# Layer 2's cross-attention output taken by token tile, with the next units' splits traced behind the norms

## The chip, the cores and the metric

The kernel runs on one core of one Trainium2 chip. The metric is the time of one execution on the device in microseconds (us); smaller is better. The core's engines work side by side, each through its own list of instructions in order: PE (the matrix engine, with its weight loads shown as PEld), DVE (vector), ACT (scalar and activation functions), POOL, and SP, whose queue issues the transfers from memory.

## The reference, cut to what matters

The program is an encoder of two layers over 256 tokens of width 1024, in float32. Each layer has a mixer, a cross-attention to a memory of 256 tokens and a feed-forward part (FFN), and each of the three ends in a residual with a layer norm:

```
for l in range(2):
    h = hybrid_mixer(x, ...)
    x = layer_norm(alpha * x + h, ln_g[l, 0], ln_b[l, 0])
    h = memory_cross_attention(x, mem, ...)        # softmax(q k^T) v, 4 heads, then o @ xa_o
    x = layer_norm(alpha * x + h, ln_g[l, 1], ln_b[l, 1])
    u, gt = split(x @ ffn_w_in)                    # 2 x 2816 columns
    h = (silu(dwconv(gt) + b) * u) @ ffn_w_out
    x = layer_norm(alpha * x + h, ln_g[l, 2], ln_b[l, 2])
```

What changes lies between `o @ xa_o` of the second layer and the first columns of its FFN.

## The kernel before, in words

**Tiles.** The 256 tokens are two tiles of 128 rows, `x[0]` and `x[1]` (tile 0 and tile 1 below; x_147 and x_148 in lists of instructions). A product against an activation needs it transposed, features on the partitions, so after each norm every 128x128 block of x is transposed by PE against an identity (`transp`, L455) into a PSUM bank `att` and copied out.

**Precision by splitting.** Each float32 operand is split in two: `hi` is the value rounded to the matrix engine's format (ACT's CAST, L276), `lo` is the rest (DVE's subtraction, L277). A product then takes three matmuls, hi·hi, hi·lo and lo·hi (`mm3`, L271 to L273).

**Units.** Weights come as units of 128x1024 (512 KB) in the fixed order in which the products use them. `prefetch` (called ahead of every step, up to `LOOK` = 7 units further than the step needs) issues a unit's transfer into one of 4 `raw` buffers from SP's queue and its split into one of 8 pairs of `hi` and `lo`. A raw buffer is free again when the unit's `lo` is done.

**Order.** A planner (`interleave`) merges generators of steps (the main line, norms, attention heads) by estimated costs, waits and free PSUM banks into one list, in which the code is traced. From the traced order a scheduler then builds each engine's list by its own estimates, so an engine's order differs locally from the traced one; SP's order is kept as traced. `add_manual_dep(..., NOSYNC)` only keeps two instructions of one engine in order.

**PSUM.** 3 banks `acc` and 5 banks `att`, each 128x512.

**The residual.** `tok_out` writes the output projection: first columns 0 to 511 of both tiles (two acc banks, units 0 to 3), then columns 512 to 1023 of tile 0 (an att bank, units 4 to 7), then the same columns of tile 1 in two pieces of 256. When a piece is complete, `ln_part` adds it to x (L391, on DVE) and takes its statistics (L396). `residual` starts the norm of tile 0 (`ln`) when `tail` = 4 steps are left, and that of tile 1 after the last. A norm is: BN_AGGR (L409), ACT's square root (L410), `sub` (L414, two pieces of 512 in tile 0, four of 256 in tile 1), a reciprocal (L426), `scale` (L419, same pieces), then the transposes (L455) and their splits into `hi` and `lo` (L276, L277).

**Behind it, in layer 2 only.** `keep_warm` (L1052) is a product of the identity with itself, 8 matmuls whose result nobody reads. `up_first` (units `fm`) computes the first 512 "up" columns of the FFN token by token, for tile 0 as soon as its transposes are there, then for tile 1. Then `ffn_in` takes the "gate" units `fg` 0 to 3 (columns 0 to 511, features on the partitions), each with 2 transposes of the finished up columns (L1080), and from column 512 on pairs of units `fu` and `fg`. Each unit's product is `proj_twin` (L299 to L303) into an acc bank, which `fold` empties (L307 on ACT, L308 on DVE). A gate unit then goes through a small convolution (L1090 on ACT, L1091, L1093 on DVE), silu (L1095, ACT) and the product with the up columns (L1096, DVE). The first silu of a layer is preceded by the load of silu's table into ACT.

## Time and profile before

| | |
|---|---|
| time, median of 3 runs | 1125.92 us (1124.89 to 1125.96) |
| the profiled execution | 1125.41 us; its span from first to last instruction is 1123.6 us |
| granted clock of the matrix engine, mean | 0.995 |
| busy share of the span | PE 98%, PEld 87%, DVE 74%, ACT 57%, POOL 1% |
| read from memory | 204.18 MB, 183 GB/s over the span |

Busy shares are of the whole span. A line such as L276 is a line of the kernel; helpers have one line for all their callers. In a timeline, a row gives the start in us from the span's start, the time until the last of the row's instructions ends, the engine, the line and operation, output and inputs by the program's names without numbers, how many, and in brackets how long the engine was idle before and what ended that. Matmuls overlap: one of 512 columns is listed with 0.39 us though the next starts 0.23 us later.

### The profile page before, as it was taken

To read this page: it belongs to the slowest core of one execution; us is meant where nothing else is said; L and a number is where in the kernel's file an instruction comes from. 1 tells how busy PE (TensorE), PEld (TensorE's weight loads), DVE (VectorE), ACT (ScalarE), POOL (GpSimd) and SP (SyncE) were. 2 spreads that over 40 slices of the span, in tenths; PEclk is the share of its full clock that TensorE was granted. 3 is DMA by queue.
4 is the path that set the end of the run, shared out by engine and by line. 5 is a ranking of instruction groups with operands and counts; after the bars stand their busy time and mean duration, and the time that the engine had idled before them with its cause. 6 is when DMAs were issued, how large, how long until landed. Compare 5 with 4: busy or idle time off the path is not lost.

```text
span 1123.6 us, 17442 instructions
## 1 busy us (share of the span) xinstructions
PE 1098.5 (98%) x6700; PEld 982.5 (87%) x6700; DVE 833.0 (74%) x1300; ACT 643.8 (57%) x1060; POOL 12.4 (1%) x18
## 2 busy tenths in 40 slices
PE   9999999999999999999999999999999978999997
PEld 8899998888998988888899999888889877888886
DVE  7888888567965898885487878865777576888744
ACT  5656667445554576665355667744536436666640
POOL 0000000000000000000000000000000000000001
PEclk9999999999999999999999999999999989999999
DMA  8884436657563575666747544656746344566651
GB/s 300 284 255 145 149 133 226 187 188 243 168 205 104 174 221 188 190 190 194 263 150 232 165 148 151 200 183 197 257 149 194 131 150 150 173 189 188 195 174 37
DMA packets 60466, 208.45 MB, mean 186 GB/s; under 512 B 7008, under 2 KB 8288, under 8 KB 60384
## 3 DMA queue, kind: packets, MB, share of 16 engines
q1 hardware_dynamic: 59952, 206.83, 57.2%
q8 instruction: 52, 0.85, 0.3%
q10 hardware_dynamic: 432, 0.52, 0.1%
q14 instruction: 30, 0.25, 0.1%
HBM read 204.18 MB, written 1.05 MB: 183 GB/s over the span
## 4 chain that ended last, share of the span: by engine, by line
PE 93%; DVE 3%; ACT 1%; DMA 1%; issue 1%; SPq 0%; DVEq 0%; ACTq 0%
PE acc L271 19%; PE acc L272 19%; PE acc L273 19%; PE acc L303 12%; PE acc L301 7%; PE att L272 4%; PE att L273 4%; PE att L271 4%; PE acc L299 2%; DVE lo L277 1%; DMA raw<-in_w_dram 1%; PE att L455 1%; PE att L666 1%; PE att L581 1%; PE att L580 1%
## 5 line engine op out<-in xcount | busy, mean ns | idle before, releaser
L277 DVE TENSOR_TENSOR lo<-raw,hi 128x1024 fp32r<-128x1024 f32 x355 | 432.3, 1223 | 187.0 <-ACT hi L276 181.9
L276 ACT CAST hi<-raw 128x1024 fp32r<-128x1024 f32 x355 | 371.4, 1051 | 224.0 <-PE acc L273 75.3
L272 PE MATMUL acc<-lo,big 128*128 128x512 f32 x584 | 229.5, 393 | 0.8 <-DVE lo L277 0.8
L271 PE MATMUL acc<-hi,big 128*128 128x512 f32 x584 | 229.4, 394 | 0.0
L273 PE MATMUL acc<-hi,big 128*128 128x512 f32 x584 | 226.7, 391 | 0.0
L271 PE MATMUL acc<-big,hi 128*128 128x256 f32 x704 | 200.2, 285 | 3.2 <-ACT big L335 2.4
L273 PE MATMUL acc<-big,lo 128*128 128x256 f32 x704 | 200.5, 285 | 0.6 <-DVE lo L277 0.6
L272 PE MATMUL acc<-big,hi 128*128 128x256 f32 x704 | 199.9, 284 | 0.2 <-DVE big L277 0.2
L303 PE MATMUL acc<-big,hi 128*128 128x512 f32 x588 | 149.2, 393 | 0.0
L271 PEld LDWEIGHTS acc<-big,hi 128*128 128x128 f32 x704 | 134.7, 192 | 4.4 <-ACT big L335 2.8
L273 PEld LDWEIGHTS acc<-big,lo 128*128 128x128 f32 x704 | 134.9, 192 | 1.2 <-DVE lo L277 1.0
L272 PEld LDWEIGHTS acc<-big,hi 128*128 128x128 f32 x704 | 134.9, 192 | 0.8 <-DVE big L277 0.4
L273 PEld LDWEIGHTS acc<-hi,big 128*128 128x128 f32 x584 | 110.0, 188 | 22.8
L272 PEld LDWEIGHTS acc<-lo,big 128*128 128x128 f32 x584 | 110.3, 189 | 21.0 <-DVE lo L277 1.1
L271 PEld LDWEIGHTS acc<-hi,big 128*128 128x128 f32 x584 | 110.1, 189 | 20.1 <-ACT t L823 0.2
L303 PEld LDWEIGHTS acc<-big,hi 128*128 128x128 f32 x588 | 105.1, 189 | 18.3
L301 PEld LDWEIGHTS acc<-big,lo 128*128 128x128 f32 x672 | 91.9, 190 | 6.7 <-ACT big L276 0.2
L301 PE MATMUL acc<-big,lo 128*128 128x256 f32 x672 | 94.1, 282 | 0.0
L272 PE MATMUL att<-lo,big 128*128 128x256 f32 (+1 forms) x228 | 72.6, 319 | 0.0
L271 PE MATMUL att<-hi,big 128*128 128x256 f32 (+1 forms) x228 | 72.4, 317 | 0.0
L273 PE MATMUL att<-hi,big 128*128 128x256 f32 (+1 forms) x228 | 72.3, 318 | 0.0
L307 ACT COPY t<-acc 128x256 f32<-128x256 f32 x84 | 31.2, 372 | 65.1 <-PE acc L303 65.1
(156 smaller groups left out, 1241.0 us busy)
## 6 DMA issues: line engine op xcount, KB each, us to landing
raw<-in_w_dram SPq DMA_DIRECT2D x355, 512.0 KB, 4.2
t<-in_bias_dram SPq DMA_DIRECT2D x16, 256.0 KB, 5.7
big<-in_ln_g_dram SPq DMA_DIRECT2D x6, 512.0 KB, 5.4
big<-in_ln_b_dram SPq DMA_DIRECT2D x6, 512.0 KB, 6.2
raw<-in_memT_dram SPq DMA_DIRECT2D x6, 512.0 KB, 4.6
big<-big SPq DMA_DIRECT2D x16, 128.0 KB, 2.3
x<-in_x_dram SPq DMA_DIRECT2D x4, 256.0 KB, 7.7
t<-in_memT_dram SPq DMA_DIRECT2D x3, 256.0 KB, 6.8
```

The costliest lines, as they stand in the source:

```text
L271: mm(o, lh, rh, start=first, stop=False)
L272: mm(o, lh, rl, start=False, stop=False)
L273: self.done = mm(o, ll, rh, start=False, stop=last)
L276: return (self.nc.scalar.copy(ah, src), self.nc.vector.tensor_tensor(out=al, in0=src, in1=rd(ah), op=ALU.subtract))
L277: self.nc.vector.tensor_tensor(out=al, in0=src, in1=rd(ah), op=ALU.subtract))
L299: mm(o, hi[:, 0], xa.both(0), start=True, stop=False)
L301: mm(o[:, S:], lo[:, k], xa.hi(k), start=False, stop=False)
L303: mm(o, hi[:, k], xa.both(k), start=False, stop=k == KT - 1)
L307: self.nc.scalar.copy(dst, o[:, S:])
L455: nc.tensor.transpose(pt[:, k], self.x[i][:, (n * h + k) * P:(n * h + k + 1) * P], self.ident)
L580: self.nc.tensor.matmul(o, q[m][:, h, t], k[m][:, h], start=True, stop=False)
L581: self.nc.tensor.matmul(o, q[m][:, h, t], k[2 + m][:, h], start=False, stop=True)
```

## The change

1. In layer 2, `tok_tiles` takes the place of `tok_out`: all 1024 columns of tile 0 first, then all of tile 1 (its last 512 columns again in two pieces of 256). `residual` gets tail = 12, so tile 0's norm is started when tile 0's eight steps are traced.
2. While that runs, `prefetch` is capped: the first cap (`until`) stands before unit fm 0, is moved to fg 0 at the start of tile 1's second half, and is lifted when `up_first` comes to tile 1 (`lift`). So the splits of fm 0 to 3, and of fg 0 on, are traced behind the norms' instructions. Tile 1's adds are kept behind the last scale of tile 0 on DVE (`behind`).
3. Silu's table: a silu of one column directly behind tile 1's square root, in both layers, in the norm ahead of the FFN.
4. `keep_warm` is gone.
5. In `ffn_in` the transposed up columns of fg 0 to 3 go into att banks instead of acc banks.

The diff, cut to its core:

```
+    def ln_part(self, i, c, acc=None, behind=False):
...
+            add = nc.vector.scalar_tensor_tensor(out=x[:, sl], in0=x[:, sl], scalar=ALPHA, in1=acc, ...)
+            if behind:
+                self.tc.add_manual_dep(add.ins, self.scaled, NOSYNC, reason="behind the first tile's norm")
+            self.urgent(add)
...
             self.urgent(nc.scalar.activation(rs, mv[:, 1:2], AF.Sqrt, bias=self.epsb, scale=1.0))
+            if i == 1 and nxt is not None and nxt[-1] == "2":
+                nc.scalar.activation(self.small(1), rs, AF.Silu)
...
-                    self.urgent(scale(h))
+                    self.scaled = self.urgent(scale(h)).ins.name
...
+    def until(self, unit):
+        self.cap = self.order.index(unit)
+
+    def lift(self, unit=None):
+        self.cap = len(self.order) if unit is None else self.order.index(unit)
+        self.prefetch(min(self.pos + self.LOOK, self.cap))
+
+    def tok_tiles(self, n, l, a):
...
+        for i in range(NT):
+            for h in range(2):
+                for c in ((0, 256), (256, 512)) if i == h == 1 else ((0, 512),):
+                    for q in range(4):
+                        def fn(*u, i=i, h=h, c=c, q=q):
...
+                            if i == h == q == 0:
+                                self.until(("fm", l, 0))
+                            if i == h == 1 and q == c[0] == 0:
+                                self.lift(("fg", l, 0))
+                            if q == 0:
+                                st["o"] = (self.acc() if h == 0 else self.att())[:, :c[1] - c[0]]
+                            part(q, i, h, c)
+                            if q == 3:
+                                self.ln_part(i, (512 * h + c[0], 512 * h + c[1]), st["o"], i == 1)
...
-            yield from self.residual(self.tok_out("xo", l, ("oT", l)), f"a{l}", xn)
             um = l == DEPTH - 1
             if um:
-                yield Step(self.keep_warm, acq=1, rel=1)
+                yield from self.residual(self.tok_tiles("xo", l, ("oT", l)), f"a{l}", xn, 12)
+            else:
+                yield from self.residual(self.tok_out("xo", l, ("oT", l)), f"a{l}", xn)
+            if um:
                 yield from self.up_first(l, xn, [f"a{l}0", f"a{l}1"])
...
-        return self.tok("fm", l, 0, xn, evac, waits)
+        steps = list(self.tok("fm", l, 0, xn, evac, waits))
+        s = steps[-4]
+        s.fn = lambda *u, fn=s.fn: (self.lift(), fn(*u))
+        return steps
...
-                    st["up"] = self.acc()[:, 0:256]
+                    st["up"] = self.att()[:, 0:256]
...
-                    self.prefetch(pos + self.LOOK)
+                    self.prefetch(min(self.pos + self.LOOK, self.cap))
```

PE has 8 matmuls less (the warm-up product), ACT two instructions more, DVE as many as before; SP's list is the same row for row, and nothing outside layer 2's stretch moves but layer 1's silu table on ACT.

**PE, from the output projection to the FFN.** att_… and acc_… are PSUM banks, hi_ and lo_ a unit's split, big_ the transposed activation. Before (att_9541 is the last piece of tile 1, acc_9618 the first fm product):

```order
L271 MATMUL att_9541<-hi_9371,big_9088 128x256
L272 MATMUL att_9541<-lo_9372,big_9088 128x256
L273 MATMUL att_9541<-hi_9371,big_9090 128x256
L455 MATMUL att_9572<-ident,x_147 128x128 x4
L1052 MATMUL att_9594<-ident 128x128 x8
L455 MATMUL att_9603<-ident,x_147 128x128 x4
L271 MATMUL acc_9618<-hi_9391,big_9568 128x512
```

Now (att_9408 is tile 0's second half, acc_9445 tile 1's first half, att_9511 the first 256-column piece of tile 1's second half; the transposes have line L462):

```order
L272 MATMUL att_9408<-lo_9374,big_9090 128x512
L273 MATMUL att_9408<-hi_9373,big_9092 128x512
L273 MATMUL acc_9445<-hi_9220,big_9092 128x512
L271 MATMUL acc_9445<-hi_9220,big_9090 128x512
L272 MATMUL acc_9445<-lo_9221,big_9090 128x512
L273 MATMUL acc_9445<-hi_9220,big_9092 128x512
L462 MATMUL att_9478<-ident,x_147 128x128 x4
L271 MATMUL att_9511<-hi_9240,big_9089 128x256
```

Tile 0's transposes moved from behind all 48 matmuls of tile 1's second half to ahead of them; only four matmuls of tile 1's first half stand between the end of tile 0's product and its transposes.

**DVE, the two norms.** Before, from the add of tile 1's last piece on (the rows lo_ are splits of units fg 0 and later ones):

```order
L391 SCALAR_TENSOR_TENSOR x_148<-x_148,att_9541 128x256
L277 TENSOR_TENSOR lo_9481<-raw_9478,hi_9480 128x1024
L277 TENSOR_TENSOR lo_9493<-raw_9490,hi_9492 128x1024
L414 SCALAR_TENSOR_TENSOR x_147<-x_147,s_9505,big_9365 128x512 x2
L396 BN_STATS s_9450<-x_148 128x6
L426 RECIPROCAL s_9506<-s_9506 128x1
L409 BN_AGGR s_9581<-s_9450 128x2
L419 SCALAR_TENSOR_TENSOR x_147<-x_147,s_9506,big_9366 128x512 x2
```

Now, from tile 0's first add on:

```order
L391 SCALAR_TENSOR_TENSOR x_147<-x_147,acc_9377 128x512
L399 BN_STATS s_9403<-x_147 128x6 x2
L391 SCALAR_TENSOR_TENSOR x_147<-x_147,att_9408 128x512
L399 BN_STATS s_9403<-x_147 128x6 x2
L412 BN_AGGR s_9436<-s_9403 128x2
L421 SCALAR_TENSOR_TENSOR x_147<-x_147,s_9436,big_9367 128x512 x2
L433 RECIPROCAL s_9437<-s_9437 128x1
L426 SCALAR_TENSOR_TENSOR x_147<-x_147,s_9437,big_9368 128x512 x2
L391 SCALAR_TENSOR_TENSOR x_148<-x_148,acc_9445 128x512
L277 TENSOR_TENSOR big_9474<-att_9478,big_9474 128x2x128
```

No split of a unit stands inside tile 0's norm any more; the splits of fm 0 to 3 follow behind it.

## The prediction

> **What bounds the kernel now.** I read the page's busy table and its chain first, then PE's waits, then the timeline of the stretch that the change touches, engine by engine.

> ```profile
> PE 1098.5 (98%) x6700; PEld 982.5 (87%) x6700; DVE 833.0 (74%) x1300; ACT 643.8 (57%) x1060; POOL 12.4 (1%) x18
> PE 93%; DVE 3%; ACT 1%; DMA 1%; issue 1%; SPq 0%; DVEq 0%; ACTq 0%
> ```

> PE is the bound, and it is full: a change that keeps PE's useful work can only win where PE waits, or works for nobody. PE's waits, longest first (engine and line that waited, whom it waited for, total us, times, longest):

> ```profile
> PE att L455 <- DVE x L419: 6.2, 1, 6.2
> PE acc L271 <- ACT big L335: 2.4, 2, 1.2
> PE acc L299 <- DVE fa L1096: 1.4, 1, 1.4
> PE acc L299 <- DVE t L308: 1.4, 2, 0.7
> ```

> The first, third and fourth lie in the changed stretch. The second does not. PE's timeline there:

> ```profile
> 915.08 0.28 PE L273 MATMUL att<-hi,big 128*128 128x256 f32 x1
> 921.56 1.09 PE L455 MATMUL att<-ident,x 128*128 128x128 f32 x4 [6.20 <-DVE x L419]
> 922.44 3.31 PE L1052 MATMUL att<-ident 128*128 128x128 f32 x16
> 925.59 0.60 PE L455 MATMUL att<-ident,x 128*128 128x128 f32 x4
> 925.95 0.49 PE L271 MATMUL acc<-hi,big 128*128 128x512 f32 x1
> ...
> 944.81 0.50 PE L299 MATMUL acc<-big,hi 128*128 128x512 f32 x1 [0.70 <-DVE t L308]
> 949.52 0.50 PE L299 MATMUL acc<-big,hi 128*128 128x512 f32 x1 [1.42 <-DVE fa L1096]
> 953.52 0.50 PE L299 MATMUL acc<-big,hi 128*128 128x512 f32 x1 [0.70 <-DVE t L308]
> 956.42 0.39 PE L299 MATMUL acc<-big,hi 128*128 128x512 f32 x1
> 959.22 0.39 PE L299 MATMUL acc<-big,hi 128*128 128x512 f32 x1
> ```

> From 915.36 (915.08 + 0.28) PE stands still for 6.20 us until tile 0's scale is done; then come four transposes at half pace (0.88 us from 921.56 to 922.44, against 0.36 from 925.59 to 925.95) and 3.15 us of the warm-up product. Behind that the gate units fg 1 to 3 and the first fu unit (953.52) lose 0.70 + 1.42 + 0.70 = 2.82 us; from 956.42 on a unit takes its plain 2.80 us.

> **The change, part by part.** The sum is kept against the start of the first fu unit, 953.52 before. Up to there PE does the same useful matmuls in both kernels.

> *Removed outright.* The warm-up product, 3.15 us of PE on the path: nothing else ran on PE in that time. With work at hand when PE resumes, nothing replaces it.

> *The gap ahead of tile 0's transposes.* It does not vanish, because the transposes now stand ahead of tile 1's second half in PE's list. When they can start follows from the end of tile 0's product and the norm's chain on DVE.

> ```profile
> 905.35 0.28 PE L271 MATMUL att<-hi,big 128*128 128x256 f32 x1
> 931.09 0.39 PE L271 MATMUL acc<-hi,big 128*128 128x512 f32 x1
> 934.04 0.39 PE L272 MATMUL acc<-lo,big 128*128 128x512 f32 x1
> ```

> Up to 905.35 both lists hold the same work on PE. From 931.09 to 934.04 lie 13 starts of 512-column matmuls, so 0.227 us each. In the new list 18 of them follow from 905.35: the 10th ends tile 0's first half (start 907.39), the 14th its second half (908.30), the 18th starts at 909.21 and ends at 909.60. The operands are there: head 3's `hi` was cast at 903.71 and its `lo` at 904.33 (below). The chain from there on has a clean copy in layer 1, where the same norm had few foreign instructions in it:

> ```profile
> 280.11 0.68 DVE L391 SCALAR_TENSOR_TENSOR x<-x,acc 128x512 f32<-128x512 f32 x1
> 281.50 1.21 DVE L277 TENSOR_TENSOR lo<-raw,hi 128x1024 fp32r<-128x1024 f32 x1
> 282.63 0.39 PE L273 MATMUL att<-hi,big 128*128 128x512 f32 x1
> 283.05 0.69 DVE L391 SCALAR_TENSOR_TENSOR x<-x,att 128x512 f32<-128x512 f32 x1 [0.35 <-PE att L273]
> 286.19 0.16 DVE L426 RECIPROCAL s<-s 128x1 f32<-128x1 f32 x1
> 286.58 1.41 DVE L419 SCALAR_TENSOR_TENSOR x<-x,s,big 128x512 f32<-128x512 f32 x2
> 903.71 0.59 ACT L276 CAST big<-att 128x512 fp32r<-128x512 f32 x1 [5.64 <-PE att L273]
> 904.33 0.69 DVE L277 TENSOR_TENSOR big<-att,big 128x512 fp32r<-128x512 f32 x1 [5.00 <-ACT big L276]
> 916.51 2.35 DVE L277 TENSOR_TENSOR lo<-raw,hi 128x1024 fp32r<-128x1024 f32 x2
> 918.77 1.41 DVE L414 SCALAR_TENSOR_TENSOR x<-x,s,big 128x512 f32<-128x512 f32 x2
> 920.73 1.35 DVE L419 SCALAR_TENSOR_TENSOR x<-x,s,big 128x512 f32<-128x512 f32 x2
> ```

> An add starts 0.42 us after the start of its last matmul (282.63 to 283.05), and an add with its two statistics holds DVE for 1.39 us (280.11 to 281.50). So tile 0's adds start at 907.81 and at 909.20 (the later of 908.72 and 907.81 + 1.39). From the second add to the scales layer 1 took 3.53 us (283.05 to 286.58), of which some 0.2 are tile 1's foreign add between reciprocal and scale: 3.33 us, so the scales start at 912.53. Transposes follow a scale's start by 0.83 us (920.73 to 921.56): 913.36. The gap is 913.36 - 909.60 = 3.76 us instead of 6.20. What made it 6.20 are the splits of later units inside the norm (the 2.35 us at 916.51 stands ahead of the `sub` at 918.77); these are behind it now.

> *The gap ahead of tile 1's transposes, a new wait.* PE has 8 transposes (about 0.9 us with their starts), 48 matmuls of 256 columns (the 18 + 48 from 905.35 to 915.08 and 0.1 on took 9.8 us; less 18 x 0.227: 5.7) and fm's 24 for tile 0 (5.45) ahead of it, and comes to it at 925.4. DVE meanwhile does, behind the scales (over at 913.9): four units' `lo` (4 x 1.17, from 2.35 for two: 4.7), `lo` of four transposed blocks (4 x 0.34: 1.4), tile 1's first add with its statistics (1.39), two more of half that width (1.4); 8.9 us, and some 0.5 of waits for ACT's casts between them: tile 1's BN_AGGR ends near 923.3.

> ```profile
> 292.63 0.25 DVE L409 BATCH_NORM_AGGREGATE s<-s 128x2 f32<-128x24 f32 x1
> 294.51 0.42 DVE L277 TENSOR_TENSOR big<-att,big 128x256 fp32r<-128x256 f32 x1
> 295.04 1.67 DVE L419 SCALAR_TENSOR_TENSOR x<-x,s,big 128x256 f32<-128x256 f32 x4
> ```

> From BN_AGGR's start to the scales are 2.41 us in layer 1, 2.07 without the foreign `lo` (0.34 to the next start), so the scales start near 925.1, the first pair of transposes half a us later (925.6), and the others as the four scales come, 0.4 apart: the last ends near 927.1, where 925.4 + 0.72 would be 926.1. That costs 1.0 us. The bounds: 0 if DVE is a us earlier, 2 if a us later.

> *The three waits in the FFN.* They come from acc banks: before, a gate unit took one for its product and one for the up columns, so the third unit waited for the fold of the first. With the up columns in att, three units' products fit, and a fold has two units' time (5.6 us). Silu's table load (1.28 us, below) sat in ACT's list between fold and fold; it now stands where ACT waits for DVE and PE. I take the whole 2.82 us, and 0.3 for the three restarts (0.50 instead of 0.39 at each start), as gone. In layer 1 the same move of the table is worth nothing: PE has no wait there over 0.5 us in the FFN, and the load's new place falls in an idle stretch of ACT.

> ```profile
> 945.26 1.28 ACT L1095 ACT_TABLE_LOAD   x1
> raw<-in_w_dram SPq DMA_DIRECT2D x355, 512.0 KB, 4.2
> DMA to landing us min/median/max: 3.2/4.2/8.5
> ```

> Covers: the splits of fm 0 to 3 end by 921.4, each before PE needs it (920.0 to 924.1), since their transfers were long in. Later transfers start later, when the raw buffers are freed: fg 0 to 3 between 917.5 and 921.4, landing by 925.6, needed from 933.1 on. The next four are issued from 930.1 on, and ACT waits for them in its list ahead of the copies that free acc banks. Worked on from 927.1: four `lo` of tile 1 on DVE and its casts on ACT to 928.2, fg 0's `hi` (1.05) to 928.9, its `lo` (1.23) to 930.1, which frees a buffer; the next units' `lo` follow 1.17 apart, so the third of the new transfers is issued at 932.4 and lands at 936.6; its cast ends at 937.7, then come fg 0's copy on ACT and its add on DVE, queued behind that unit's `lo` (to 939.1): fg 0's bank is free at 939.6. PE wants it at 933.1 + 3 x 2.80 + 0.2 = 941.7: 2.1 us of slack.

> *Sum.* Lost time in the stretch before: 6.20 + 3.15 + 0.52 (cold transposes) + 2.82 + 0.3 = 12.99 us. After: 3.76 + 0.1 (its restart) + 1.0 = 4.86 us. Gain 8.1 us. Behind 953.52 PE runs without such waits to the end, in the same order, so the gain stays. Against the profiled execution, 1125.41 us (span 1123.6 and 1.8 around it): 1117.3 us; the runs' median is 0.5 above that execution. I forecast 1117.3.

> **The rivals.**

> *The clock drops in the 3.76 us gap.* The granted clock (the third column from the right) before:

> ```profile
> 918.40:918.50 0.10, 0.00 (x0) 0.00 (x0) 0.10 (x1) 0.00 (x0) 0.00 (x0) 0.82 1.20 492
> 918.50:918.60 0.10, 0.00 (x0) 0.00 (x0) 0.10 (x1) 0.00 (x0) 0.00 (x0) 0.50 0.21 82
> 925.20:925.30 0.10, 0.10 (x3) 0.10 (x2) 0.10 (x2) 0.00 (x0) 0.00 (x0) 0.54 0.00 0
> ```

> It fell to half at 918.46, 3.1 us into the idle time, and came back at 925.29, 3.7 us after PE resumed. Gaps of up to 1.42 us left it alone. A gap of 3.76 lies beyond the one case that dropped; against it stands that one case does not tell whether 3.1 us is a threshold or where a clock's tick happened to fall. If it falls, some 3.7 us of PE's work run at half pace, a loss of 1.9; tile 1's norm moves only 0.3, so its 1.0 us gap is swallowed: net +0.9, 1118.2. If it stays low for the whole 6.83 us between the two changes, the loss is 3.4 - 1.0 = 2.4: 1119.7.

> [...]

> *The FFN's waits stay in another form.* ACT's list holds casts that wait for transfers, with the acc-freeing copies behind them. Landing took up to 8.5 us in this trace; above 6.3 the slack of 2.1 is used up. For it speaks that four transfers fall together; against it the median of 4.2. Price up to the 2.82 removed: 1120.1.

> *Slower: the capped units starve PE.* The splits of fg 0 to 3 come behind tile 1's norm on ACT and DVE (fg 0's `lo` near 930.1, wanted at 933.1). Each us by which they come later than 3 us past this plan costs a us on PE; it decides at 3 + 8.1 = 11.1 us of lateness, for instance if the transfers of four units took turns and each landed in 8.5. Then 1126 or more. Against it: their raw buffers are freed from 917.5 on, 15 us before the need.

> **How the numbers follow.** Forecast (gap of about 3.8 us, full clock, no FFN waits) 0.48; clock drops 0.32; FFN waits stay, alone or with the clock, 0.15; slower 0.03; gap smaller than worked out 0.02. The range 1115.2 to 1120.8 takes the forecast with 2 us of error in the two DVE chains downwards and the rivals' 1119.7 and 1120.1 upwards. Two tenths of a per cent are 2.25 us, about what a measurement of this kernel can tell from no change: faster means under 1123.7, which all cases give but the slower one (0.03) and losing cases that add up (0.04 of their 0.47).

> **What would show it.** Right: PE idle once, 3.5 to 4 us, ahead of the transposes of tile 0 (L462); no L1052; a short wait at tile 1's; no wait over 0.5 us on L299 after it; the table load behind a square root. Wrong: clock at half behind that gap; ACT's casts waiting for transfers while a copy (L307) is late; idle PE ahead of fm or fg 0 for a `lo`.

## The result, and the profile after

The changed kernel takes 1118.44 us (median of 4 runs, 1117.51 to 1118.91), the kernel before beside it 1125.62 (4 runs): a ratio of 0.9934, 95% interval 0.9922 to 0.9947. It is faster by 7.2 us; 8.1 were forecast. The profiled execution took 1118.29 us.

The page's span and busy table, then the two longest of PE's waits (engine and line that waited, whom it waited for, total us, times, longest):

```profile
span 1116.5 us, 17399 instructions
PE 1096.6 (98%) x6684; PEld 980.5 (88%) x6684; DVE 831.6 (74%) x1300; ACT 643.2 (58%) x1062; POOL 12.3 (1%) x18
```

```profile
PE att L462 <- DVE x L426: 3.7, 1, 3.7
PE acc L271 <- ACT big L335: 2.4, 2, 1.2
```

Ahead of tile 0's transposes PE now waits 3.7 us instead of 6.2; the second row is the wait outside the stretch that was there before. L299, with three waits before, is not in the list any more. PE's timeline in the stretch:

```profile
908.77 0.39 PE L273 MATMUL acc<-hi,big 128*128 128x512 f32 x1
912.90 1.11 PE L462 MATMUL att<-ident,x 128*128 128x128 f32 x4 [3.74 <-DVE x L426]
...
917.01 0.41 PE L271 MATMUL att<-hi,big 128*128 128x256 f32 x1
917.23 0.42 PE L272 MATMUL att<-lo,big 128*128 128x256 f32 x1
...
919.09 0.28 PE L271 MATMUL att<-hi,big 128*128 128x256 f32 x1
919.21 0.28 PE L272 MATMUL att<-lo,big 128*128 128x256 f32 x1
...
927.80 1.03 PE L462 MATMUL att<-ident,x 128*128 128x128 f32 x8
934.89 0.62 PE L299 MATMUL acc<-big,hi 128*128 128x512 f32 x2
940.62 0.47 PE L299 MATMUL acc<-big,hi 128*128 128x512 f32 x1
943.64 0.48 PE L299 MATMUL acc<-big,hi 128*128 128x512 f32 x1
946.52 0.39 PE L299 MATMUL acc<-big,hi 128*128 128x512 f32 x1
```

One gap is left, 3.74 us from 909.16 to 912.90. Tile 1's transposes (927.80) follow without a wait, and so do the FFN's units: fg 0 and 1 start together at 934.89, fg 2 and 3 at 940.62 and 943.64, the first fu unit at 946.52. But matmuls of 256 columns start 0.22 us apart at 917 and 0.12 apart at 919: behind the gap the clock was at half. In the table by stretches (bounds, length, then busy time of PE, PEld, DVE, ACT and POOL; the third column from the right is the granted clock):

```profile
912.10:912.20 0.10, 0.00 (x0) 0.00 (x0) 0.10 (x1) 0.00 (x0) 0.00 (x0) 0.97 0.00 0
919.00:919.10 0.10, 0.10 (x3) 0.10 (x3) 0.10 (x1) 0.10 (x2) 0.00 (x0) 0.90 0.59 246
```

Worked out from the shares in these rows, the clock fell at 912.19, 3.0 us into the gap, and came back at 919.02: 6.83 us low, of which PE worked 6.1.

DVE's timeline shows the norm of tile 0 without foreign splits, and the four `lo` of fm behind it (three from 916.27, one at 920.01, not shown):

```profile
908.78 0.67 DVE L391 SCALAR_TENSOR_TENSOR x<-x,att 128x512 f32<-128x512 f32 x1
910.27 0.26 DVE L412 BATCH_NORM_AGGREGATE s<-s 128x2 f32<-128x24 f32 x1
910.57 1.41 DVE L421 SCALAR_TENSOR_TENSOR x<-x,s,big 128x512 f32<-128x512 f32 x2
912.09 1.42 DVE L426 SCALAR_TENSOR_TENSOR x<-x,s,big 128x512 f32<-128x512 f32 x2
916.27 3.50 DVE L277 TENSOR_TENSOR lo<-raw,hi 128x1024 fp32r<-128x1024 f32 x3 [0.40 <-ACT hi L276]
926.00 1.67 DVE L426 SCALAR_TENSOR_TENSOR x<-x,s,big 128x256 f32<-128x256 f32 x4
```

ACT loads silu's table behind tile 1's square root, and its casts in the FFN wait for transfers, the longest 2.00 us, without a copy that PE needs being late:

```profile
924.27 1.28 ACT L417 ACT_TABLE_LOAD   x1
935.48 1.05 ACT L276 CAST hi<-raw 128x1024 fp32r<-128x1024 f32 x1 [2.00 <-DMA raw<-in_w_dram]
```

**A ruler for all kernels.** To keep differences upstream out, I measure from the last transposes of the attention heads, which stand ahead of everything that changes, to the start of the first fu unit. Their rows in PE's timeline, before and then after:

```profile
896.01 0.49 PE L900 MATMUL att<-ident,t 128*128 128x128 f32 x3
```

```profile
895.58 0.49 PE L907 MATMUL att<-ident,t 128*128 128x128 f32 x3
```

The stretch was 953.52 - 896.01 = 57.51 us and is 946.52 - 895.58 = 50.94: 6.57 us gained in it. The profiled executions differ by 7.12; 0.43 of the rest is an earlier start of the stretch, and 0.12 lies behind it. The 0.43 us are not the change's: 0.28 of them are there 36 us into the span, ahead of all that differs, and between two kernels that are alike up to the stretch (after, and after with the up columns in acc) its start differs by 1.31 us.

### The profile page after: what moved, and what is told of

Its sections match the earlier page's. It is cut to its first block, busy times and chain, and to the rows that moved or that the text cites. A ratio compares the mean times of both kernels' runs of the same rounds, so it can differ in the third digit from the quotient of the medians.

```text
span 1116.5 us, 17399 instructions
## 1 busy us (share of the span) xinstructions
PE 1096.6 (98%) x6684; PEld 980.5 (88%) x6684; DVE 831.6 (74%) x1300; ACT 643.2 (58%) x1062; POOL 12.3 (1%) x18
## 3 DMA queue, kind: packets, MB, share of 16 engines
HBM read 204.18 MB, written 1.05 MB: 184 GB/s over the span
## 4 chain that ended last, share of the span: by engine, by line
PE 91%; DVE 3%; DMA 2%; ACT 1%; SPq 1%; issue 1%; DVEq 0%; ACTq 0%
PE acc L271 18%; PE acc L272 18%; PE acc L273 18%; PE acc L303 12%; PE acc L301 7%; PE att L272 4%; PE att L273 4%; PE att L271 4%; PE acc L299 2%; DMA raw<-in_w_dram 1%; PE att L462 1%; DMA big<-in_emb_ln_b_dram 1%; DVE lo L277 1%; PE att L673 1%; PE att L588 1%
## 5 line engine op out<-in xcount | busy, mean ns | idle before, releaser
L277 DVE TENSOR_TENSOR lo<-raw,hi 128x1024 fp32r<-128x1024 f32 x355 | 432.1, 1223 | 179.3 <-ACT hi L276 173.6
L276 ACT CAST hi<-raw 128x1024 fp32r<-128x1024 f32 x355 | 371.2, 1052 | 221.7 <-PE acc L273 72.8
L272 PE MATMUL acc<-lo,big 128*128 128x512 f32 x584 | 229.5, 393 | 0.8 <-DVE lo L277 0.8
L271 PE MATMUL acc<-hi,big 128*128 128x512 f32 x584 | 229.0, 394 | 0.4 <-ACT hi L276 0.4
L273 PE MATMUL acc<-hi,big 128*128 128x512 f32 x584 | 227.0, 391 | 0.0
L271 PE MATMUL acc<-big,hi 128*128 128x256 f32 x704 | 200.5, 286 | 3.2 <-ACT big L335 2.4
L273 PE MATMUL acc<-big,lo 128*128 128x256 f32 x704 | 200.8, 285 | 0.6 <-DVE lo L277 0.6
L272 PE MATMUL acc<-big,hi 128*128 128x256 f32 x704 | 200.2, 285 | 0.2 <-DVE big L277 0.2
L271 PEld LDWEIGHTS acc<-big,hi 128*128 128x128 f32 x704 | 134.8, 192 | 4.4 <-ACT big L335 2.8
L273 PEld LDWEIGHTS acc<-big,lo 128*128 128x128 f32 x704 | 135.0, 192 | 1.2 <-DVE lo L277 1.0
L272 PEld LDWEIGHTS acc<-big,hi 128*128 128x128 f32 x704 | 135.0, 192 | 0.8 <-DVE big L277 0.4
L273 PEld LDWEIGHTS acc<-hi,big 128*128 128x128 f32 x584 | 109.8, 188 | 22.8 <-DVE big L277 0.2
L272 PEld LDWEIGHTS acc<-lo,big 128*128 128x128 f32 x584 | 110.0, 188 | 21.7 <-DVE lo L277 1.9
L271 PEld LDWEIGHTS acc<-hi,big 128*128 128x128 f32 x584 | 109.8, 188 | 20.9 <-ACT hi L276 1.0
L272 PE MATMUL att<-lo,big 128*128 128x256 f32 (+1 forms) x228 | 73.8, 324 | 0.0
L271 PE MATMUL att<-hi,big 128*128 128x256 f32 (+1 forms) x228 | 73.5, 322 | 0.0
L273 PE MATMUL att<-hi,big 128*128 128x256 f32 (+1 forms) x228 | 73.4, 322 | 0.0
L307 ACT COPY t<-acc 128x256 f32<-128x256 f32 x84 | 31.1, 370 | 59.0 <-PE acc L303 59.0
## 6 DMA issues: line engine op xcount, KB each, us to landing
raw<-in_w_dram SPq DMA_DIRECT2D x355, 512.0 KB, 4.3
big<-in_ln_g_dram SPq DMA_DIRECT2D x6, 512.0 KB, 5.4
big<-in_ln_b_dram SPq DMA_DIRECT2D x6, 512.0 KB, 6.2
raw<-in_memT_dram SPq DMA_DIRECT2D x6, 512.0 KB, 4.7
```

What stands on the lines that cost most here:

```text
L271: mm(o, lh, rh, start=first, stop=False)
L272: mm(o, lh, rl, start=False, stop=False)
L273: self.done = mm(o, ll, rh, start=False, stop=last)
L276: return (self.nc.scalar.copy(ah, src), self.nc.vector.tensor_tensor(out=al, in0=src, in1=rd(ah), op=ALU.subtract))
L277: self.nc.vector.tensor_tensor(out=al, in0=src, in1=rd(ah), op=ALU.subtract))
L307: self.nc.scalar.copy(dst, o[:, S:])
```

## The experiments

Each was timed beside the kernel before on the same chip; "stretch" is the ruler's, from one profiled execution. The chips differ from batch to batch; the kernel before took 1125.62 to 1126.06 us on them, so times of two experiments compare to about half a us. Two theories stood from the start. Mine: the gain is the sum of two separate things, PSUM banks for the FFN's waits, and DVE's list (what stands ahead of tile 0's scale) for the gap; the clock takes some back. Against it: the tile order itself, the removed product or the table does it.

### The FFN's waits

**Up columns in acc again** (the changed kernel otherwise):

```
-                    st["up"] = self.att()[:, 0:256]
+                    st["up"] = self.acc()[:, 0:256]
```

> Edit: the changed kernel with the transposed up columns of fg 0 to 3 in acc banks again. Theory (the three waits of the FFN came from two acc banks per gate unit): waits of 1.4 to 2.8 us in all come back on the first matmul of a unit, 1120 to 1121. Rival (they came from the splits and the table load between the folds on ACT and DVE, and are gone with these): 1118.4.

1124.81 us (11 runs; ratio to before 0.9992, 0.9983 to 1.0001); the stretch 55.83, 4.9 longer than after. PE's timeline:

```profile
943.60 0.50 PE L299 MATMUL acc<-big,hi 128*128 128x512 f32 x1 [2.98 <-DVE t L308]
948.73 0.50 PE L299 MATMUL acc<-big,hi 128*128 128x512 f32 x1 [0.29 <-DVE fa L1141]
952.72 0.50 PE L299 MATMUL acc<-big,hi 128*128 128x512 f32 x1 [0.70 <-DVE t L308]
```

The waits are back, 3.97 us of them instead of 2.82, and by time nothing measurable is left of the gain, some 4 us more than I expected to lose. Of the 6.3 us between the two profiled executions 1.3 stand ahead of the stretch, where the kernels are alike, and 4.9 in it. The gate units stand closer together on PE now (fg 0 and 1 start at 934.40 and 937.35; before at 934.26 and 940.84), and without the banks the third waits the longer. The longest wait also cost the clock, which is seen in the table by stretches:

```profile
944.40:944.50 0.10, 0.10 (x3) 0.10 (x2) 0.10 (x1) 0.10 (x1) 0.00 (x0) 0.97 1.46 451
```

It fell to half at 944.49, 0.9 us after PE had resumed, for 3.4 us. In return it was low for 3.4 us instead of 6.83 behind the gap ahead of tile 0 (from 913.78, not shown). So the 4.9 us are not the price of the waits alone.

**The banks alone, on the kernel before**, and **banks and early table on the kernel before** (the second has the second line too):

```
-                    st["up"] = self.acc()[:, 0:256]
+                    st["up"] = self.att()[:, 0:256]
+            if i == 1 and nxt is not None and nxt[-1] == "2":
+                nc.scalar.activation(self.small(1), rs, AF.Silu)
```

> The kernel before with one line changed: the transposed up columns of fg 0 to 3 in att banks; the table load stays between two folds on ACT. Theory (the banks alone make the FFN's waits): no wait on L299 over 0.5 us, 3.8 us less, 1121.5, as with the early table. Rival (the table load of 1.28 us holds a fold up by itself): one wait of 0.5 to 1.3 us stays on L299: 1122.2 to 1122.8.

> Edit: the kernel before with the transposed up columns in att banks and silu's table loaded behind tile 1's square root, nothing else. Theory (these two made the FFN's three waits, 2.82 us): 1125.6 - 2.8 = 1122.8. Rival (the waits hang on the folds being late behind the splits, which this does not move): 1125.6.

The banks alone: 1122.72 us (7 runs; 0.9970, 0.9959 to 0.9981). With the table: 1121.46 (0.9962, 0.9949 to 0.9976). In both no wait on L299 is listed. The banks alone took the time that the rival gave (1122.2 to 1122.8), but the wait that it rests on is not there. PE's timeline and ACT's with the banks alone:

```profile
935.31 0.39 PE L299 MATMUL acc<-big,hi 128*128 128x512 f32 x1
950.95 0.47 PE L299 MATMUL acc<-big,hi 128*128 128x512 f32 x1
```

```profile
946.30 1.28 ACT L1095 ACT_TABLE_LOAD   x1
```

From fg 0's start to the first fu unit are 15.64 us here and 15.65 with the early table, against 19.26 before (934.26 to 953.52): 3.62 us for the banks, though the load still stands between two folds. The two kernels' stretches differ by 1.22 us (54.92 and 53.70), ahead of the FFN, by the clock: it fell at 920.64 and at 917.39 for 6.83 us each, with PE idle to 921.59 and to 920.93, so 5.9 us of PE's work ran cold in the first and 3.3 in the second. The medians differ by 1.3, with intervals that overlap.

**The changed kernel with the late table:**

```
-            if i == 1 and nxt is not None and nxt[-1] == "2":
+            if False:
```

> Edit: the changed kernel without the early silu, so that the table load (1.28 us) stands ahead of the first silu again, in both layers. Theory (a fold has over 2 us of slack in the changed kernel, which takes the load in): 1118.4, no wait on the first matmul of a unit. Rival (the load holds up the folds behind it): up to 1.4 us more, 1119.8.

1118.07 us (0.9930, 0.9918 to 0.9943), no wait on L299; the load is back in the FFN:

```profile
946.44 1.28 ACT L1140 ACT_TABLE_LOAD   x1
```

Early or late, the table is worth nothing that these runs can tell. This kernel's stretch is even 1.27 us shorter than after, since here the clock was low for 3.4 us instead of 6.83, and its time is the same within what a measurement can tell. The early table has a small price of its own, which I had not seen: tile 1's reciprocal overwrites in place what the early silu reads, so it waits until the load and the silu are over, 0.17 us in the changed kernel (L433 at 925.80, behind L417) and not at all here.

### The clock and the warm-up product

**PE kept busy in the gap**: 14 matmuls of the identity with itself (two records each), as in the removed warm-up, ahead of tile 0's transposes.

```
+            if nxt == "xt12" and i == 0 and h == 0:
+                self.warm(14, self.done)
```

> Edit: the changed kernel with 14 matmuls of the identity with itself (some 2.7 us at full clock) between the last matmul of tile 1's first half and tile 0's transposes, inside the 3.74 us gap. Theory (the clock fell in that gap and PE worked some 6 us at half pace, a loss near 3 us of which 1 us comes back as a wait ahead of tile 1's transposes): the granted clock stays at 1.00, and the time falls by about 2 us against the changed kernel's 1118.4, to 1116.4. Rival (the identity product does not hold the clock, or the half clock was hidden behind DVE's norms anyway): 1118.4, unchanged.

1116.73 us (0.9918, 0.9905 to 0.9932), 1.7 less than after (the intervals overlap, but its slowest run, 1117.17, is below the fastest of after, 1117.51); the stretch is 48.63, 2.3 less. PE's timeline (the product is L531):

```profile
909.64 3.29 PE L531 MATMUL att<-ident 128*128 128x128 f32 x28
913.63 0.63 PE L464 MATMUL att<-ident,x 128*128 128x128 f32 x4 [0.69 <-DVE x L426]
926.13 1.14 PE L464 MATMUL att<-ident,x 128*128 128x128 f32 x6 [0.21 <-DVE x L426]
```

The granted clock stays at full (1.00 from 900 to 945 us), and the first transposes take 0.63 instead of 1.11 us. The product computes nothing, and tile 0's transposes start no earlier for it (17.41 us into the stretch, 17.32 after): what it buys is the clock alone. At full clock PE waits at tile 1's transposes, but 0.21 us, not the 1.0 forecast.

**The warm-up product dropped from the kernel before:**

```
-                yield Step(self.keep_warm, acq=1, rel=1)
```

> Edit: the kernel before without its warm-up product, nothing else. If the prediction's term stands by itself (3.15 us of PE on the path): 1125.6 - 3.15 = 1122.5. Rival (the fm product waits for the casts of the transposes and for a lo that stands behind tile 1's sub on DVE until 924.1, and PE's first matmuls then run at half clock): 0.5 us won at most, 1125.1 to 1125.6.

1124.57 us (11 runs; 0.9985, 0.9976 to 0.9994); 1.5 below the kernel before beside it and between the two expectations; the stretch 56.34, 1.17 less than before instead of 3.15. The transposes behind the 6.20 us gap in PE's timeline, and the 8 us around them in the table by stretches:

```profile
922.73 1.94 PE L455 MATMUL att<-ident,x 128*128 128x128 f32 x8 [6.20 <-DVE x L419]
```

```profile
920.00:928.00 8.00, 5.27 (x18) 4.28 (x19) 7.47 (x20) 1.50 (x5) 0.00 (x0) 0.57 0.41 133
```

The clock was at half from 920.89 to 927.71, and with the dummy work gone 5.0 us of it fell on transposes and fm's product. Of the product's 3.15 us, 2.85 had stood in time at half clock (922.44 to 925.29) that somebody has to sit through.

### The gap: the cap, the tile order, DVE's list

**No cap** (later units' splits traced as early as `LOOK` allows):

```
     def until(self, unit):
-        self.cap = self.order.index(unit)
+        pass
     def lift(self, unit=None):
-        self.cap = len(self.order) if unit is None else self.order.index(unit)
+        self.cap = len(self.order)
```

> Edit: the changed kernel without the cap, so that prefetch runs 7 units ahead as before. The splits of fm 2 and 3 then stand inside tile 0's norm on DVE, those of fg 0 to 2 inside tile 1's. Theory (the splits inside the norm made the gap of before): tile 0's transposes come 2.3 us later, a gap of about 6 us again, clock at half behind it; 1118.4 + 2 = 1120.5. Rival (the order by token tile does it alone, the cap is worth nothing): 1118.4.

1122.27 us (6 runs; 0.9971, 0.9959 to 0.9982); the stretch 54.00, 3.1 longer than after. DVE's timeline, then PE's:

```profile
908.89 1.22 DVE L277 TENSOR_TENSOR lo<-raw,hi 128x1024 fp32r<-128x1024 f32 x1
...
911.27 1.22 DVE L277 TENSOR_TENSOR lo<-raw,hi 128x1024 fp32r<-128x1024 f32 x1
```

```profile
915.82 1.12 PE L462 MATMUL att<-ident,x 128*128 128x128 f32 x4 [5.76 <-DVE x L426]
930.80 1.23 PE L462 MATMUL att<-ident,x 128*128 128x128 f32 x6 [1.42 <-DVE x L426]
933.46 0.50 PE L273 MATMUL acc<-hi,big 128*128 128x512 f32 x1 [0.64 <-DVE big L277]
```

Two `lo` of 1.22 us between tile 0's adds and their statistics make the gap 5.76 instead of 3.74, and further ones delay tile 1. The loss is above the 2 us that I expected: 3.8 by time, 3.1 in the stretch. Part of it is the early table, as DVE's timeline shows ahead of tile 1's scales:

```profile
930.06 0.16 DVE L433 RECIPROCAL s<-s 128x1 f32<-128x1 f32 x1 [1.11 <-ACT s L417]
```

On ACT a unit's cast came between the square root (to 927.58) and the load (from 928.53), so the reciprocal waits 1.11 us here instead of 0.17. So the 3.1 us are the price of the cap with the early table in place; what the cap is worth without the table no run shows.

**The old order of columns with everything else changed** (cap, banks, table, no warm-up product):

```
+    def tok_cols(self, n, l, a, first):
+        for k, s in enumerate(self.tok_out(n, l, a)):
+            if k == 0:
+                s.fn = lambda *u, fn=s.fn: (self.until(first), fn(*u))
+            if k == 8:
+                s.fn = lambda *u, fn=s.fn: (self.lift(("fg", l, 0)), fn(*u))
+            yield s
...
-                yield from self.residual(self.tok_tiles("xo", l, ("oT", l)), f"a{l}", xn, 12)
+                yield from self.residual(self.tok_cols("xo", l, ("oT", l), ("fm", l, 0)), f"a{l}", xn)
```

> The changed kernel with the output projection in the old order again (first columns of both tiles, then the second half of tile 0, then that of tile 1), but with the cap on later units, the att banks and the early table kept, and without the warm-up product. Theory (DVE's list of work between the product and the first FFN unit is the bound, not the order of the tiles): PE now ends the whole projection before it waits, at about 915; tile 0's scales stand behind tile 1's last add, near 915.9, so a first wait of about 1.3 us; then fm 0 waits for the lo of tile 0's blocks behind four lo of fm units (4.7 us), a second wait of about 5 us; none at tile 1. 6.4 us lost against 12.99 before and no FFN waits: about 1118.7, the same as the changed kernel. Rival (the tile order is what shortens the norm): with the old order the gap stays near 6 us and a wait at fm 0 is added to it: 1121.5 or more.

1120.35 us (5 runs; 0.9951, 0.9939 to 0.9964); the stretch 51.99, 1.1 longer than after. PE's timeline, then the DVE row behind its last wait:

```profile
916.57 1.29 PE L462 MATMUL att<-ident,x 128*128 128x128 f32 x8 [1.27 <-DVE x L426]
918.20 0.50 PE L271 MATMUL acc<-hi,big 128*128 128x512 f32 x1 [0.34 <-ACT big L276]
922.34 0.79 PE L273 MATMUL acc<-hi,big 128*128 128x512 f32 x1 [3.41 <-DVE big L277]
```

```profile
918.48 3.48 DVE L277 TENSOR_TENSOR lo<-raw,hi 128x1024 fp32r<-128x1024 f32 x3
```

The time lies between the two expectations (1118.7 and 1121.5 or more). The mechanism is the theory's: with the cap the old order has no gap near 6 us either; PE waits 1.27 us for the scale as worked out, then 0.34 + 3.41 for the `lo` of tile 0's blocks, which stands behind the fm splits (5 expected). That makes 5.02 us of waits against 3.74, and the clock fell here too (to half, from 920.10 to 926.93). So the tile order is worth about 1.1 of the 6.6 us in the stretch (1.3 by the waits, 1.9 by time); the cap and the banks carry more.

**Tile 0's transposes later on PE** (behind the first 24 matmuls of tile 1's second half):

```
-                yield Spawn(f"{name}0", self.ln(0, xn, 1 if name[0] != "f" else 0, 4.4))
+                yield Spawn(f"{name}0", self.ln(0, xn, 1 if name[0] != "f" else 0, 6.0 if tail == 12 else 4.4))
```

> Edit: the planner takes tile 0's norm for longer (6.0 instead of 4.4), so that tile 0's transposes stand behind the first 24 matmuls of tile 1's second half in PE's list. Theory A (DVE's chain through both norms and the splits of fm 0 to 3 sets the end of the stretch): the gap ahead of tile 0's transposes shrinks to about 0.9 us, but PE then waits about 0.9 us for the first fm split and about 3 us ahead of tile 1's transposes; no gap reaches the 3.1 us that dropped the clock; 1116.3, the same as with the identity product. Rival B (PE's order is what costs, and the 2.9 us taken out of the gap are won besides the clock): 1112.5 to 1113.5.

1117.76 us (0.9927, 0.9914 to 0.9941); the stretch 49.83. PE's timeline, then DVE's row of tile 0's first add:

```profile
914.73 1.29 PE L462 MATMUL att<-ident,x 128*128 128x128 f32 x8 [2.19 <-DVE x L426]
922.08 0.50 PE L273 MATMUL acc<-hi,big 128*128 128x512 f32 x1 [2.72 <-DVE big L277]
```

```profile
909.12 0.69 DVE L391 SCALAR_TENSOR_TENSOR x<-x,acc 128x512 f32<-128x512 f32 x1 [4.04 <-PE acc L273]
```

With 24 matmuls more to cover the gap, PE still stands idle for 4.91 us. The gap did not close, its time moved behind the transposes, to a `lo` that waits for DVE. The clock stayed at full (1.00 from 900 to 945 us). The edit did more than its text says: in PE's list matmuls of tile 1 now stand among those of tile 0, so tile 0's first add starts 13.05 us into the stretch instead of 11.81. Those 1.24 us are about what the time lies above theory A's 1116.3 and the first wait above its 0.9. The expectation that the gap merely needs cover (1112.5 to 1113.5) is refuted even so.

**The same with two fm splits ahead of tile 0's norm**, where DVE has idle time:

```
-                                self.until(("fm", l, 0))
+                                self.until(("fm", l, 2))
```

> Edit: as the run with the later transposes, and the first cap is put behind unit fm 1 instead of ahead of fm 0, so that the splits of fm 0 and fm 1 stand on DVE ahead of tile 0's norm, where DVE was idle for 2.8 us. Theory A (DVE's chain is the bound): 2 x 1.17 = 2.3 us leave the chain between the norms: 2.3 us less than the run with the later transposes, about 1114.0. Rival B (PE's order is the bound): no change against that run. Rival C (the two splits, 2.4 us with their casts, do not fit into the idle time and push tile 0's norm): less than 1 us won.

1114.83 us (4 runs; 0.9903, 0.9889 to 0.9916), the fastest of all, 3.6 below the changed kernel; the stretch 47.14. DVE's timeline, then PE's:

```profile
905.01 2.36 DVE L277 TENSOR_TENSOR lo<-raw,hi 128x1024 fp32r<-128x1024 f32 x2 [0.26 <-ACT hi L276]
908.80 0.69 DVE L391 SCALAR_TENSOR_TENSOR x<-x,acc 128x512 f32<-128x512 f32 x1 [1.43 <-PE acc L273]
```

```profile
914.40 1.29 PE L462 MATMUL att<-ident,x 128*128 128x128 f32 x8 [2.18 <-DVE x L426]
```

Two splits moved into time in which DVE waits for PE anyway (after them it is still idle for 1.43 us), and the wait for `lo` is gone: 2.9 us less by time than with the later transposes alone (2.7 in the stretch), 2.3 expected. Tile 0's first add starts 13.05 us into the stretch here too, so that is not what differs. What bounds the stretch is the length of DVE's list from tile 0's first add on. The cap on all four fm units is too strict, on none too loose.

## Why the prediction was right, and where not

The time came out inside the range, on the right side, 1.1 us above the forecast, but by way of a rival: **the clock dropped in the gap**, which the prediction gave a chance of 0.32 and 1118.2 to 1119.7. Its steps in their order:

- *The gap.* 3.76 forecast, 3.74 measured. Its chain holds link by link: the stretch began 0.43 us earlier than before, and the scales, expected at 912.53, started at 912.09, 0.44 earlier.
- *Cover and cap.* No wait at fm or fg 0; the units behind the cap were in time.
- *The FFN's waits.* Gone, as forecast, and through the banks. The term was 2.82 + 0.3; alone it measures 3.62. The three waits stand ahead of fg 2, fg 3 and the first fu unit (not fg 1 to 3, as the reading of the timeline has it), and from a unit's start to the next they cost 0.85, 1.69 and 0.97 us against the same steps with the banks alone, where 0.70, 1.42 and 0.70 are listed as idle. The table load was misread: in the middle of the folds it costs PE nothing, and in its new place, taken for idle time, it holds up tile 1's reciprocal.
- *Slack for the transfers.* 2.1 us were worked out on ACT and DVE; casts did wait up to 2.00 us for transfers, and PE never noticed. This rival did not come.
- *Tile 1's wait.* 1.0 forecast, none measured, because a cold PE came later (927.80 instead of 925.4) than DVE's scales (926.00 instead of 925.1). At full clock it was 0.21: over-estimated.
- *The warm-up product, "removed outright", 3.15 us.* This is the step that failed as stated. Nothing replaces the product only if PE has its clock when it resumes. By itself its removal gave 1.17 us. In the sum it stood as a whole, beside the 0.52 of cold transposes, which belongs to the same low clock: both were taken as gained, as if the low clock went away with the product.
- *The clock.* The last row that I had (a fall 3.1 us into a gap of 6.20) already lay inside 3.74, and the gap held a fall in each of the three kernels that had it (after, late table, up columns in acc). A chance of 0.32 was too low, and no run shows it: before, the stretch had one gap of over 1.42 us, and the clock fell in it; the runs showed a fall in every profile with a gap of 3.41 us or more, nine with the two of before and after. The time is not the rival's by its own sum either: the clock was low for 6.83 us, the case priced at 1119.7. That it came out at 1118.4 is some 0.5 us more from the FFN's waits than the term held, 0.5 from outside the stretch, and a cold loss of 3.0 (worked out below) instead of 3.4.

With the FFN's waits at their measured 3.62 us the sum closes: 13.5 lost before; after, 3.74 + 0.1; and 13.5 - 6.57 - 3.84 = 3.1 us are left for the clock. PE's starts in the cold time give as much: behind the gap 21 matmuls of 256 columns start 0.225 us apart instead of 0.119, and 8 transposes 0.184 instead of 0.09 (four in 0.36 us before), 3.0 us in all. Keeping PE warm brought 2.3 of them; part of the rest is the wait at tile 1 that a warm PE has (0.21 us and a restart). The forecast's miss would have been larger, 1.5 in the stretch, but for 0.5 us outside it that the change did not make.

## What to carry to other kernels

Where PE waits on a chain through DVE, list what DVE executes between the first and the last link and move the rest into DVE's own idle time; more cover on PE only moves the wait, and a reordering on PE is worth what it shortens of that list. Before counting a product of dummy work as pure loss, ask whose clock it keeps, and where it stands: such work placed inside the gap of 3.74 us gained 1.7 us, while the same kind of work behind a gap of 6.20 us stood mostly in time that was cold anyway. Count PSUM banks per unit in flight first: one word in the code carried 3.6 of the microseconds. And before moving work into an engine's idle time, look for what another engine overwrites or reads behind it: the table load, moved into ACT's idle time, kept DVE waiting for up to 1.11 us.

## What the runs showed of the hardware

The last 3.41 us before a fall, in three kernels (banks and table on the kernel before; up columns in acc, its second fall; the old order of columns):

```profile
913.98:917.39 3.41, 0.75 (x7) 0.54 (x5) 3.41 (x7) 1.91 (x3) 0.00 (x0) 1.00 0.60 211
```

```profile
941.08:944.49 3.41, 0.90 (x6) 0.85 (x7) 3.38 (x6) 2.26 (x5) 0.00 (x0) 1.00 0.81 243
```

```profile
916.69:920.10 3.41, 1.87 (x10) 0.99 (x9) 3.41 (x5) 1.46 (x3) 0.00 (x0) 1.00 0.14 29
```

PE was listed as busy for a fifth, a quarter and over half of them (0.75, 0.90 and 1.87 us), so in these three kernels the last 3.41 us before a fall were not idle throughout.

PE's listed busy time does not draw the line either. The banks alone on the kernel before had less of it than the 1.87 us in the second last 3.41 us before their fall, and kept the clock through them:

```profile
913.81:917.22 3.41, 1.57 (x14) 1.37 (x12) 3.41 (x8) 2.74 (x4) 0.00 (x0) 1.00 0.65 161
```

What separates these four rows is the number of columns in the matmuls started within them: 1024, 1792 and at most 1920 in the three ahead of a fall, 2816 in the one that kept the clock (the 1.87 us were mostly transposes, of 128 columns each, the 1.57 us matmuls of 256). In the profiles of the kernels before and after I counted these columns in every 3.413 us at full clock, laid off from the fall in the gap, from 20 to 1105 us, 315 times in each. The one ahead of the fall had 256 columns before and 0 after; all others had at least 3328 before and 3840 after; without waits 3.413 us take some 7700 (512 per 0.227 us). The count does not decide wherever it is taken: with tile 0's transposes later on PE, 3.40 us with 1536 columns (three matmuls of 512, 918.70 to 922.10, not shown) kept the clock at 1.00. If it decides on such a tick, with the line between 1920 and 2816, a gap of 3.74 us loses the clock in 6 to 8 of 10 positions of the tick (an estimate from these counts and the 7700), so that it did in all three kernels with such a gap would be partly chance. No run here varied the count by itself.
